# A two-layer hybrid encoder on one core: state-space maps issued in smaller steps, and sums, divisions and neighbours in the mixer rearranged

## The chip, the cores and the metric

The kernel runs on one core of a Trainium2 chip. The metric is device time in microseconds. The core has TensorE (PE in the rows, its weight loads PEld), VectorE (DVE), ScalarE (ACT), GpSimd (POOL) and SyncE (SP), which here only issues DMAs. Each engine works through a queue of its own, in order.

## The reference

The input x is 512 x 1024, float32; two layers, each with four residual steps, then a final RMSNorm:

```python
x = x + 0.5 * swiglu(rms_norm(x, ffn1_norm[i]), w_gate, w_up, w_down)     # d_ff = 2816
q, k, v, u = split(rms_norm(x, mix_norm[i]) @ w_in[i])                    # 512, 128, 128, 512 columns
attn = banded_attention(q, k, v, sink, bias)        # 8 heads, 2 kv heads, |i-j| <= 128, blocks of 128
ssm = s5_mixer(u, ...)                              # 32 groups of 16 channels, 64 complex states, 2 directions
x = x + concat(rms_norm(attn), rms_norm(ssm)) @ w_out[i]
x = x + 0.5 * swiglu(rms_norm(x, ffn2_norm[i]), ...)
```

The state-space mixer steps s_t = A s_(t-1) + B u_t and reads y_t = Re(C s_t), with a diagonal complex A for each group, once forwards and once backwards; y passes a GELU and a gated linear unit.

## The kernel before, in words

Activations are held transposed (channels on the 128 partitions, 512 tokens along the free axis). Float32 accuracy comes from three passes (`mm3`, L227 to L231): each weight chunk of 128 x 2048 is loaded to `raw`, ACT rounds it to `whi` (L212), and DVE or POOL subtracts to get `wlo` (L215), in halves of 1024 columns. `POOL_SPLIT` lists the halves that POOL takes, as (kind, first tile, half).

**The feed-forward blocks** (`ffn`, L364) run three groups of 8, 7 and 7 tiles of 128 hidden channels. A tile is 48 matmuls (gate and up, 8 x 3 each); after a group come 8 down tiles of 24 or 21. The down result is added to x (L421, L423), on POOL except in the last group.

**The maps of the state-space mixer** (`s5_steps`, L530) are computed from the parameters in the background of the feed-forward blocks. The function is a generator: each `yield` ends a step. `set_bg` (L164) gives it so many steps for so many points; a gate-and-up tile counts 3 points, a down tile 1, and `step` (L169) runs the generator until it has kept pace. Layer 0's generator (with the attention bias first) gets 224 steps for the 90 points of the first block, layer 1's 180 for 150 points of the two blocks between the mixers. What is left is drained before the mixer. In order, the generator makes scalars and powers, tables of cosines and sines (L669 to L694, POOL), and then eight units u (L717 to L777) of four groups. A unit makes, on POOL, the output map f (`fr`, `fi`, L734 to L737, from Cr, Ci and the powers pf) and the input map e (`er`, `ei`, L741 to L744, from four factors that DMAs have brought back from `bt` and `pt` in DRAM), 12 instructions on 128 x 512; e goes to `ed` in DRAM, f a unit later (`LAG = 1`) into TensorE products (L757, L764) with the padded B and then to `fd`.

**The mixer** (`mixer`, L800) runs the steps that `ORDER` (L45) lists by hand. `pu` projects u, `ui` brings it back from DRAM in another layout (8 DMAs a tile), `l` loads a quarter's input maps and tables (4 `ed`, 3 `tb` DMAs), `L` its output maps; `si` (L866) applies the input map on TensorE and rotates by the tables (L880 to L887), `sc` (L890) scans on DVE (L894) and rotates back (L897 to L908), `so` (L912) applies the output map. `k`, `v`, `vt` and `q` are the projections of attention, `as` the scores of a unit (block n, kv head) with the exponential on ACT, `an` the division of the probabilities (L1035), `ao` transposes them (L1043 to L1048), `pv` multiplies by v and squares for the norm (L1053 to L1076). `yt`, `glu` and `sn` end the state-space branch; `ws` and then `wa` are the two halves of the output projection (L1099, L1109), each adding to x at L1113; `ADD_V` says which of these adds are DVE's (first for ws, then for wa). After each wa add, `after(d)` prepares the next block's input (L290, L296, L301, L308).

The program is traced in this order, and a scheduler then fixes each engine's queue, taking what it expects to be ready first; so an engine's order in the trace need not be the program's. Activations and temporaries share one pool of slots that `slot` hands out (L105).

Of the kernel before, what the change touches and what calls it, by code (L numbers as in the profile page):

```python
# [12 lines left out]
AF = mybir.ActivationFunctionType  # L13
ALU = mybir.AluOpType
# [3 lines left out]
P = 128  # L18
# [27 lines left out]
l0 ui0 pu2 pu3 ui2 si0 ui1 k l1 ui3 v vt si1 L0 q0 sc0 sc1 l2 q1 si2 q2 l3 si3 sc2 q3 L1 L3 so0 L2 as0 an0  # L46
as1 so1 sc3 so2 so3 yt0 yt1 an1 as2 ao0 an2 as4 ao1 glu pv0 as3 ao2 sn ws0 an4 an3 ao3 ws1 as5 ws2 ao4 ws3
an5 as6 an6 ws4 ws5 ao5 pv1 as7 ws6 an7 ao6 pv2 ao7 ws7 pv3
""".split()

POOL_SPLIT = {("u", 0, 0), ("u", 0, 1), ("u", 2, 0), ("q", 0, 0), ("q", 0, 1), ("q", 2, 1), ("glu", 0, 1),
              ("ws", 0, 1), ("ws", 4, 0), ("wa", 0, 1), ("wa", 4, 1)}
# [3 lines left out]
ADD_V = ((0, 7), (5, 7))  # L56
# [22 lines left out]
class Emit:  # L79
# [450 lines left out]
    def s5_steps(self, l):  # L530
# [186 lines left out]
        for u in range(8 + LAG):  # L717
            if u < 8:
                g0 = u * 4
                fac = nxt  # L720

                def mat(x):
                    return x[:, g0 * 16:g0 * 16 + 64].rearrange("p (g o h) -> p g o h", g=4, o=1).to_broadcast([P, 4, 8, 16])

                def pwo(x, r):
                    return x[:, r, :, g0:g0 + 4].rearrange("p n (g o) -> p g n o", o=1).to_broadcast([P, 4, 8, 16])

                def full(x):
# [71 lines left out]
    def mixer(self, l, st, after):  # L800
# [65 lines left out]
        def s_in(q):  # L866
# [157 lines left out]
        def a_norm(n, kv):  # L1024
# [7 lines left out]
            for i in range(4):  # L1032
                hd = kv * 4 + i
                p = at[n]["p"][kv][:, i * T:i * T + nk]
                V.tensor_scalar(p, p, den[:, hd:hd + 1], None, op0=M)  # L1035

        def a_out(n, kv):
            k0, k1 = at[n]["k"]
            pp = at[n]["p"].pop(kv)
            for kb in range(k0, k1):  # L1040
# [4 lines left out]
                if kb % 2:  # L1045
# [7 lines left out]
        def a_pv(n):  # L1053
# [309 lines left out]
def plan_all(e):  # L1363
    st = new_st(GC_FFN1)
    e.setup(st)
    for l in range(L):
# [6 lines left out]
        if l == 0:  # L1373
            e.set_bg(prep(), 224, 90)
# [5 lines left out]
        if l + 1 < L:  # L1380
            e.set_bg(e.s5_steps(l + 1), 180, 150)
# [23 lines left out]
```

## Time and profile before

| | us |
|---|---|
| median of 3 runs | 1917.55 (1916.8 to 1920.2) |
| profiled execution, its own time | 1919.46 |
| its span, first to last instruction | 1917.7 |
| busy: TensorE, DVE, POOL, ACT | 1853.3, 1095.9, 690.9, 618.3 |

A time in a row counts from the start of the span. Layer 0's first block ends near 405 us, its mixer near 606; layer 1's mixer lies between about 1343 and 1540 us. Where a row ends in brackets, it gives the idle time just before the instruction and what ended it. "PEclk" is the granted clock of TensorE as a share of 2.4 GHz.

### The profile page before, as it was taken

The numbers are of one execution on the slowest core, as the hardware profiler recorded it, in microseconds if no ns is written. First come the engines' busy times: TensorE is split into PE (matmuls) and PEld (weight loads), VectorE is DVE, ScalarE is ACT, GpSimd is POOL, SyncE is SP. The second block draws the span as 40 slices with busy tenths as digits, with TensorE's granted clock in tenths as the row PEclk, the third lists the DMA queues.
The fourth block names the chain that finished last, engine by engine and source line by source line (L and its number), as shares of the span: only waits on it lengthen the run. The fifth ranks groups of instructions, "written<-read, shape, count | busy, mean of one in ns | idle before, by whom it ended". The sixth has DMA issues, their size and how long they took to land. (4 is left out here: it accounts for less than half of the span.)

```text
span 1917.7 us, 23722 instructions
## 1 busy us (share of the span) xinstructions
PE 1853.3 (97%) x9360; PEld 1500.3 (78%) x9360; DVE 1095.9 (57%) x1724; ACT 618.3 (32%) x932; POOL 690.9 (36%) x581
## 2 busy tenths in 40 slices
PE   8999997998999999999999999999989999999997
PEld 6888885887667888888888888888776678888886
DVE  7655542659876846345664444446598663434435
ACT  5222221332743322223332122224247442222223
POOL 2029878644244015074483551103343320201102
PEclk9999998999899999999999999999999999999998
DMA  5534546666221223334434433525650122232321
GB/s 203 165 123 140 178 158 204 187 241 221 72 69 66 109 88 140 110 115 160 157 144 149 173 134 103 152 88 184 199 179 23 66 86 91 88 107 83 107 96 47
DMA packets 95799, 249.46 MB, mean 130 GB/s; under 512 B 31768, under 2 KB 39112, under 8 KB 79944
## 3 DMA queue, kind: packets, MB, share of 16 engines
q1 hardware_dynamic: 94456, 246.86, 38.4%
q8 instruction: 73, 1.20, 0.3%
q10 hardware_dynamic: 1232, 1.09, 0.2%
q14 instruction: 38, 0.31, 0.0%
HBM read 217.89 MB, written 36.32 MB: 133 GB/s over the span
## 5 line engine op out<-in xcount | busy, mean ns | idle before, releaser
L229 PE MATMUL psum<-blk,whi 128*128 128x512 f32 (+1 forms) x2446 | 952.7, 391 | 11.6 <-ACT blk L290 6.5
L230 PE MATMUL psum<-blk,whi 128*128 128x512 f32 (+1 forms) x2446 | 952.2, 390 | 6.1 <-DVE blk L296 5.9
L231 PE MATMUL psum<-blk,wlo 128*128 128x512 f32 (+1 forms) x2446 | 951.2, 390 | 1.2 <-DVE wlo L215 1.2
L229 PEld LDWEIGHTS psum<-blk,whi 128*128 128x128 f32 x2446 | 460.5, 188 | 111.9 <-ACT blk L290 6.7
L230 PEld LDWEIGHTS psum<-blk,whi 128*128 128x128 f32 x2446 | 460.6, 188 | 104.2 <-DVE blk L296 10.7
L231 PEld LDWEIGHTS psum<-blk,wlo 128*128 128x128 f32 x2446 | 460.5, 188 | 96.1 <-DVE wlo L215 2.1
L212 ACT CAST whi<-raw 128x1024 fp32r<-128x1024 f32 (+1 forms) x310 | 303.3, 1027 | 714.3 <-PE psum L230 492.9
L215 DVE TENSOR_TENSOR wlo<-raw,whi 128x1024 fp32r<-128x1024 f32 (+1 forms) x288 | 411.9, 1463 | 83.7 <-ACT whi L212 74.8
L397 DVE TENSOR_TENSOR blk<-psum,blk 128x512 f32<-128x512 f32 x88 | 60.7, 691 | 315.0 <-PE psum L231 308.3
L423 POOL TENSOR_TENSOR xtile<-xtile,blk 128x512 f32<-128x512 f32 x64 | 92.5, 1447 | 392.9 <-DVE blk L421 344.1
L421 DVE SCALAR_TENSOR_TENSOR blk<-psum,blk 128x512 f32<-128x512 f32 x94 | 64.8, 690 | 190.8 <-PE psum L231 179.9
L396 ACT ACTIVATE blk<-blk 128x512 f32<-128x512 f32 x88 | 55.6, 632 | 325.3 <-DVE blk L394 321.4
L394 DVE TENSOR_TENSOR blk<-psum,blk 128x512 f32<-128x512 f32 x88 | 60.3, 689 | 107.4 <-PE psum L231 79.6
L215 POOL TENSOR_TENSOR wlo<-raw,whi 128x1024 fp32r<-128x1024 f32 x22 | 59.0, 2689 | 132.1 <-ACT whi L212 77.5
L308 POOL TENSOR_TENSOR blk<-blk,blk 128x512 f32<-128x512 f32 x30 | 46.3, 1543 | 132.5 <-ACT blk L301 131.8
L401 DVE TENSOR_TENSOR blk<-blk,blk 128x512 fp32r<-128x512 f32 x88 | 72.2, 822 | 0.1
L296 DVE SCALAR_TENSOR_TENSOR blk<-xtile,consts,blk 128x512 fp32r<-128x512 f32 x48 | 58.5, 1237 | 9.9 <-ACT blk L290 9.9
L1113 POOL TENSOR_TENSOR xtile<-xtile,blk 128x512 f32<-128x512 f32 x24 | 34.0, 1439 | 73.4 <-DVE blk L1111 73.4
L308 POOL TENSOR_TENSOR blk<-blk 128x512 f32<-128x512 f32 x11 | 17.5, 1591 | 110.8 <-issue 87.1
L735 POOL TENSOR_TENSOR blk<-blk,blk 128x512 f32<-128x512 f32 x32 | 44.1, 1380 | 30.5 <-DVE blk L401 26.1
L400 ACT CAST blk<-blk 128x512 fp32r<-128x512 f32 x88 | 54.1, 615 | 2.7 <-DVE blk L397 2.7
L290 ACT ACTIVATE blk<-xtile,consts 128x512 fp32r<-128x512 f32 x48 | 34.2, 719 | 51.5 <-DVE xtile L423 37.5
(235 smaller groups left out, 1388.3 us busy)
## 6 DMA issues: line engine op xcount, KB each, us to landing
raw<-w SPq DMA_DIRECT2D x123, 1024.0 KB
raw<-w SPq DMA_DIRECT2D x32, 896.0 KB
blk<-pt SPq DMA_DIRECT2D x32, 256.0 KB
blk<-bt SPq DMA_DIRECT2D x32, 256.0 KB
fd<-blk SPq DMA_DIRECT2D x32, 256.0 KB
ed<-blk SPq DMA_DIRECT2D x32, 256.0 KB
blk<-ed SPq DMA_DIRECT2D x32, 256.0 KB
blk<-fd SPq DMA_DIRECT2D x32, 256.0 KB
```

The lines of the kernel that those rows point to most:

```text
L212: self.S.copy(hi[:, c], raw[:, c])
L215: eng.tensor_tensor(out=lo[:, c], in0=raw[:, c], in1=hi[:, c].bitcast(F32), op=ALU.subtract)
L229: t.matmul(out, wh, xh, start=start, stop=False)
L230: t.matmul(out, wh, xl, start=False, stop=False)
L231: t.matmul(out, wl, xh, start=False, stop=stop)
L296: self.V.scalar_tensor_tensor(lo.bitcast(F32R), self.x[d], self.gains[:, st["g"] + d:st["g"] + d + 1], hi, op0=ALU.mult, op1=ALU.subtract)
L308: eng.tensor_tensor(out=acc, in0=acc, in1=sq, op=ALU.add)
L394: V.tensor_tensor(out=s, in0=pg, in1=R, op=ALU.mult)
L397: V.tensor_tensor(out=s, in0=pu, in1=s, op=ALU.mult)
L401: V.tensor_tensor(out=lo.bitcast(F32R), in0=s, in1=hi, op=ALU.subtract)
L421: V.scalar_tensor_tensor(t, ps, 0.5, R, op0=ALU.mult, op1=ALU.mult)
L423: (V if last else self.G).tensor_tensor(out=self.x[d], in0=self.x[d], in1=t, op=ALU.add)
```

## The change

In the maps, a unit makes e first and f after it; each of the 12 POOL instructions now ends with a yield of its own, f's slots are taken later, and the factor loads of the next unit are issued between e and f as before between e and the next unit's f. The steps given are 256 (layer 0) and 212 (layer 1). In the order, l1 moves behind ui3 and v, ws4 ahead of an6, pv1 behind as7, ws6 and an7, and ws7 behind pv3. Work changes engines: four sums of `si` go from POOL to DVE, five divisions a layer from DVE to ACT, the last sum of squares of n = 0 to DVE, three halves of weight splits from POOL to DVE; of the ws adds d = 0 and 7 go to POOL and d = 4 to DVE, and the wa adds d = 5 and 7 go to POOL. `G_SUM` and `V_PT` write out what the code did already.

```diff
-l0 ui0 pu2 pu3 ui2 si0 ui1 k l1 ui3 v vt si1 L0 q0 sc0 sc1 l2 q1 si2 q2 l3 si3 sc2 q3 L1 L3 so0 L2 as0 an0
+l0 ui0 pu2 pu3 ui2 si0 ui1 k ui3 v l1 vt si1 L0 q0 sc0 sc1 l2 q1 si2 q2 l3 si3 sc2 q3 L1 L3 so0 L2 as0 an0
 as1 so1 sc3 so2 so3 yt0 yt1 an1 as2 ao0 an2 as4 ao1 glu pv0 as3 ao2 sn ws0 an4 an3 ao3 ws1 as5 ws2 ao4 ws3
-an5 as6 an6 ws4 ws5 ao5 pv1 as7 ws6 an7 ao6 pv2 ao7 ws7 pv3
+an5 as6 ws4 an6 ws5 ao5 as7 ws6 an7 pv1 ao6 pv2 ao7 pv3 ws7

-POOL_SPLIT = {("u", 0, 0), ("u", 0, 1), ("u", 2, 0), ("q", 0, 0), ("q", 0, 1), ("q", 2, 1), ("glu", 0, 1),
-              ("ws", 0, 1), ("ws", 4, 0), ("wa", 0, 1), ("wa", 4, 1)}
+G_SIN = {(1, 1), (2, 0), (3, 0), (3, 1)}
+G_SUM = {(0, 1), (1, 1), (2, 1)}
+G_SQ = {(0, 0), (1, 0), (1, 1), (2, 0), (2, 1)}
+V_PT = {(0, 1), (0, 3), ... (7, 1), (7, 3)}
+S_DIV = {(3, 0), (3, 2), (5, 1), (6, 2), (7, 1)}
+POOL_SPLIT = {("glu", 0, 1), ("q", 0, 1), ("u", 0, 0), ("u", 0, 1), ("wa", 0, 1), ("wa", 4, 1), ("ws", 0, 1),
+              ("ws", 4, 0)}

-ADD_V = ((0, 7), (5, 7))
+ADD_V = ((4,), ())

-                fr, fi, er, ei, t = (self.slot() for _ in range(5))
+                er, ei, t = (self.slot() for _ in range(3))
                 M = ALU.mult
-                for o, a, b, sg in ((fr, Cr, Ci, ALU.add), (fi, Ci, Cr, ALU.subtract)):
-                    Gp.tensor_tensor(out=full(o), in0=mat(a), in1=pwo(pfv, 0), op=M)
-                    Gp.tensor_tensor(out=full(t), in0=mat(b), in1=pwo(pfv, 1), op=M)
-                    yield
-                    Gp.tensor_tensor(out=o, in0=o, in1=t, op=sg)
-                    yield
                 b0, b1, p0, p1 = fac
                 for r, (o, a, b, sg) in enumerate(((er, b0, b1, ALU.subtract), (ei, b1, b0, ALU.add))):
                     Gp.tensor_tensor(out=o, in0=a, in1=p0, op=M)
+                    yield
                     Gp.tensor_tensor(out=t, in0=b, in1=p1, op=M)
                     yield
                     Gp.tensor_tensor(out=o, in0=o, in1=t, op=sg)
                     SP.dma_start(out=ed[u // 2, :, r, u % 2 * T:u % 2 * T + T], in_=o)
                     yield
-                self.free(t, er, ei, *fac)
+                self.free(er, ei, *fac)
                 if u < 7:
                     nxt = factors(u + 1)
+                fr, fi = self.slot(), self.slot()
+                for o, a, b, sg in ((fr, Cr, Ci, ALU.add), (fi, Ci, Cr, ALU.subtract)):
+                    Gp.tensor_tensor(out=full(o), in0=mat(a), in1=pwo(pfv, 0), op=M)
+                    yield
+                    Gp.tensor_tensor(out=full(t), in0=mat(b), in1=pwo(pfv, 1), op=M)
+                    yield
+                    Gp.tensor_tensor(out=o, in0=o, in1=t, op=sg)
+                    yield
+                self.free(t)

-            Gp.tensor_tensor(out=s[0], in0=s[0], in1=s[1], op=A)
+            (Gp if (q, 0) in G_SIN else V).tensor_tensor(out=s[0], in0=s[0], in1=s[1], op=A)
-            Gp.tensor_tensor(out=s[2], in0=s[3], in1=s[2], op=B)
+            (Gp if (q, 1) in G_SIN else V).tensor_tensor(out=s[2], in0=s[3], in1=s[2], op=B)

-                V.tensor_scalar(p, p, den[:, hd:hd + 1], None, op0=M)
+                if (2 * n + kv, i) in S_DIV:
+                    S.activation(p, p, AF.Copy, scale=den[:, hd:hd + 1])
+                else:
+                    V.tensor_scalar(p, p, den[:, hd:hd + 1], None, op0=M)

-            e.set_bg(prep(), 224, 90)
+            e.set_bg(prep(), 256, 90)
-            e.set_bg(e.s5_steps(l + 1), 180, 150)
+            e.set_bg(e.s5_steps(l + 1), 212, 150)
```

## Rows read from the trace of the kernel before

**Rows 1.** The page, busy time, share of the span and instructions of TensorE.

```profile
PE 1853.3 (97%) x9360; PEld 1500.3 (78%) x9360; DVE 1095.9 (57%) x1724; ACT 618.3 (32%) x932; POOL 690.9 (36%) x581
```

**Rows 2.** TensorE's waits: waiting line, releaser, us in total, times, longest.

```profile
PE psum L757 <- POOL blk L737: 13.6, 2, 8.0
...
PE psum L1010 <- DVE blk L881: 6.4, 2, 3.2
...
PE psum L985 <- DVE blk L961: 5.0, 2, 3.3
...
PE psum L229 <- ACT blk L1069: 2.4, 2, 1.2
```

**Rows 3.** Busy time by stretch: length, PE, PEld, DVE, ACT, POOL, clock, DMA.

```profile
142.00:192.00 50.00, 50.00 (x222) 41.42 (x221) 24.93 (x25) 13.88 (x17) 48.91 (x78) 1.00 0.46 144
192.00:298.00 106.00, 106.00 (x581) 86.92 (x580) 49.32 (x46) 22.60 (x31) 86.35 (x62) 1.00 0.55 169
298.00:313.00 15.00, 1.36 (x18) 0.57 (x20) 3.84 (x3) 2.67 (x4) 12.49 (x12) 0.66 0.62 206
313.00:364.00 51.00, 50.41 (x319) 40.44 (x312) 27.05 (x27) 14.37 (x23) 45.47 (x32) 0.97 0.54 183
```

**Rows 4.** Timeline of TensorE, 302 to 313 us: start, us, then the operation.

```profile
303.96 0.65 PE L757 MATMUL psum<-blk,blk 128*32 128x128 f32 x8 [5.64 <-POOL blk L737]
312.61 0.66 PE L757 MATMUL psum<-blk,blk 128*32 128x128 f32 x8 [8.00 <-POOL blk L737]
```

**Rows 5.** The table by stretch again, right after the stall.

```profile
312.00:316.00 4.00, 3.39 (x30) 2.84 (x31) 0.00 (x0) 0.00 (x0) 2.70 (x3) 0.50 0.58 195
```

**Rows 6.** POOL's groups, 192 to 313 us: busy, mean ns, idle before.

```profile
L423 POOL TENSOR_TENSOR xtile<-xtile,blk 128x512 f32<-128x512 f32 x8 | 11.7, 1472 | 0.0
L741 POOL TENSOR_TENSOR blk<-blk,blk 128x512 f32<-128x512 f32 x8 | 11.4, 1425 | 13.1 <-DMA blk<-bt 10.9 <-issue 2.2
```

**Rows 7.** The table by stretch in layer 0's mixer and just before it.

```profile
430.00:488.00 58.00, 49.90 (x467) 40.16 (x467) 53.13 (x75) 14.36 (x20) 32.74 (x21) 0.90 0.67 220
536.00:560.00 24.00, 24.00 (x106) 15.85 (x104) 17.17 (x51) 8.82 (x24) 10.12 (x6) 0.93 0.12 44
392.00:424.00 32.00, 32.00 (x153) 26.76 (x152) 18.18 (x25) 9.13 (x13) 11.56 (x5) 1.00 0.74 264
```

**Rows 8.** Timeline of DVE in layer 0's mixer, 434 to 444 us.

```profile
435.66 2.29 DVE L894 TENSOR_TENSOR_SCAN blk<-blk,blk 128x511 f32<-128x511 f32 x1 [0.97 <-POOL blk L884]
...
438.12 0.69 DVE L903 TENSOR_TENSOR blk<-blk,blk 128x512 f32<-128x512 f32 x1
438.73 1.22 DVE L894 TENSOR_TENSOR_SCAN blk<-blk,blk 128x511 f32<-128x511 f32 x1
439.87 2.80 DVE L906 TENSOR_TENSOR blk<-blk,blk 128x512 f32<-128x512 f32 x1
...
443.80 1.21 DVE L215 TENSOR_TENSOR wlo<-raw,whi 128x1024 fp32r<-128x1024 f32 x1
```

**Rows 9.** Timeline of POOL, 439 to 442 us.

```profile
439.78 2.34 POOL L215 TENSOR_TENSOR wlo<-raw,whi 128x1024 fp32r<-128x1024 f32 x1 [2.91 <-ACT whi L212]
```

**Rows 10.** Timeline of SP's DMA issues in layer 1's mixer, 1372 to 1380 us.

```profile
1373.38 0.43 SPq L851 DMA_DIRECT2D blk<-ed  x1
1373.85 5.39 SPq L823 DMA_DIRECT2D blk<-ud  x8
```

**Rows 11.** Timeline of TensorE in layer 1's mixer, 1376 to 1382 us.

```profile
1378.96 0.45 PE L875 MATMUL psum<-blk,blk 128*64 128x64 f32 x6 [1.35 <-DMA blk<-ed]
1381.11 0.80 PE L985 MATMUL psum<-consts,blk 128*128 128x128 f32 x4 [1.71 <-DVE blk L961]
```

**Rows 12.** The page's groups: an ACT pass over 128 x 512.

```profile
L396 ACT ACTIVATE blk<-blk 128x512 f32<-128x512 f32 x88 | 55.6, 632 | 325.3 <-DVE blk L394 321.4
```

**Rows 13.** Timeline of POOL at the end of layer 0's mixer, 594 to 600 us.

```profile
594.76 5.51 POOL L1113 TENSOR_TENSOR xtile<-xtile,blk 128x512 f32<-128x512 f32 x4 [17.94 <-DVE blk L1111]
```

**Rows 14.** Timeline of DVE at the same place, 607 to 610 us.

```profile
607.54 1.77 DVE L1113 TENSOR_TENSOR xtile<-xtile,blk 128x512 f32<-128x512 f32 x1
```

More of the change, by code (lines that the diff above doesn't have):

```diff
@@ L45 @@
 ORDER = """
-l0 ui0 pu2 pu3 ui2 si0 ui1 k l1 ui3 v vt si1 L0 q0 sc0 sc1 l2 q1 si2 q2 l3 si3 sc2 q3 L1 L3 so0 L2 as0 an0
+l0 ui0 pu2 pu3 ui2 si0 ui1 k ui3 v l1 vt si1 L0 q0 sc0 sc1 l2 q1 si2 q2 l3 si3 sc2 q3 L1 L3 so0 L2 as0 an0
 as1 so1 sc3 so2 so3 yt0 yt1 an1 as2 ao0 an2 as4 ao1 glu pv0 as3 ao2 sn ws0 an4 an3 ao3 ws1 as5 ws2 ao4 ws3
-an5 as6 an6 ws4 ws5 ao5 pv1 as7 ws6 an7 ao6 pv2 ao7 ws7 pv3
+an5 as6 ws4 an6 ws5 ao5 as7 ws6 an7 pv1 ao6 pv2 ao7 pv3 ws7
 """.split()
-POOL_SPLIT = {("u", 0, 0), ("u", 0, 1), ("u", 2, 0), ("q", 0, 0), ("q", 0, 1), ("q", 2, 1), ("glu", 0, 1),
-              ("ws", 0, 1), ("ws", 4, 0), ("wa", 0, 1), ("wa", 4, 1)}
+G_SIN = {(1, 1), (2, 0), (3, 0), (3, 1)}
+G_SUM = {(0, 1), (1, 1), (2, 1)}
+G_SQ = {(0, 0), (1, 0), (1, 1), (2, 0), (2, 1)}
+V_PT = {(0, 1), (0, 3), (1, 1), (1, 3), (2, 1), (2, 3), (3, 1), (3, 3), (4, 1), (4, 3), (5, 1), (5, 3), (6, 1),
+        (6, 3), (7, 1), (7, 3)}
+S_DIV = {(3, 0), (3, 2), (5, 1), (6, 2), (7, 1)}
+POOL_SPLIT = {("glu", 0, 1), ("q", 0, 1), ("u", 0, 0), ("u", 0, 1), ("wa", 0, 1), ("wa", 4, 1), ("ws", 0, 1),
+              ("ws", 4, 0)}
 POOL_Q = ((2, 1), (3, 1))
-ADD_V = ((0, 7), (5, 7))
+ADD_V = ((4,), ())
 STARTX = ((0, 1), (1, 1), (2, 2), (4, 2), (6, 2))
@@ L904, in s_scan @@
             V.tensor_tensor(out=s[2], in0=s[3], in1=si, op=M)
-            both(V, rho, s[0], s[2], B)
+            both(Gp if (q, 0) in G_SUM else V, rho, s[0], s[2], B)
             V.tensor_tensor(out=s[1], in0=s[1], in1=si, op=M)
             V.tensor_tensor(out=s[3], in0=s[3], in1=co, op=M)
-            both(V if q == 3 else Gp, co, s[1], s[3], A)
+            both(Gp if (q, 1) in G_SUM else V, co, s[1], s[3], A)
             self.free(*s, si)
@@ L1044, in a_out @@
                 pt = self.slot()
-                if kb % 2:
+                if (2 * n + kv, kb) in V_PT:
                     V.tensor_copy(pt, b)
@@ L1072, in a_pv @@
             V.tensor_tensor(out=abuf[1][:, cs].bitcast(F32R), in0=f, in1=abuf[0][:, cs], op=B)
-            eng = V if n == 3 else Gp
-            eng.tensor_tensor(out=q[:, 0:256], in0=q[:, 0:256], in1=q[:, 256:512], op=A)
-            eng.tensor_tensor(out=acc_a[:, n * P:(n + 1) * P], in0=q[:, 0:P], in1=q[:, P:2 * P], op=A)
+            eng = [Gp if (n, i) in G_SQ else V for i in range(2)]
+            eng[0].tensor_tensor(out=q[:, 0:256], in0=q[:, 0:256], in1=q[:, 256:512], op=A)
+            eng[1].tensor_tensor(out=acc_a[:, n * P:(n + 1) * P], in0=q[:, 0:P], in1=q[:, P:2 * P], op=A)
             self.free(f, q, at[n]["sm"])
```

## The prediction

> **What bounds the kernel now.** First the page's busy line: TensorE counts 1853.3 us of a span of 1917.7 [rows 1], so 64.4 us are idle; only these, and stretches at a lowered clock, can be won. Next TensorE's waits [rows 2]: the largest that this change touches is that of L757 (the state-space maps' products) for POOL's sums in L737, 13.6 us in two waits; then, in the mixers, waits for DVE (L881, L961) and for ACT at L1069. The start and the end of the program make most of the rest, and the change leaves them alone.
>
> The table by stretch places the large wait: in 298 to 313 us TensorE is busy 1.36 us of 15, and POOL is nearly full from 142 us on: 48.91 of 50 us, 86.35 of 106, then 12.49 of 15 in the stall itself [rows 3]. TensorE's rows say the same: the fifth product (unit 4) waited 5.64 us for its real part and 8.00 for its imaginary part [rows 4]. Afterwards the granted clock is 0.50, the lower level of 1.2 GHz, in 312 to 316 us, with 3.39 us of TensorE work [rows 5], so 1.7 us more are lost. The stall's whole price is 13.6 + 1.7 = 15.3 us, once: layer 1's maps are spread over 150 points, not 90, and show no such wait.
>
> **Part 1: maps in smaller steps, input maps first.** No POOL instruction is added or removed (12 a unit, 8 units). What moves is when they are issued. Counting yields in layer 0: 26 for the bias, 51 to the tables, 32 for the tables, 2, then the units (88 before, 120 after), 14 at the end: 213 and 245. The pace is 224/90 = 2.49 and 256/90 = 2.84 steps a point, so all ends near point 86 in both. But the tables begin at 77/2.84 = 27.1 instead of 30.9 points, the units at 111/2.84 = 39.0 instead of 44.6. A point of a gate-and-up tile is 16 matmuls; at 222 matmuls in 50 us [rows 3] that is 3.6 us, and one of a down tile is 24, so 5.4 us. Both starts come some 20 us earlier (5.6 x 3.6; 3.8 x 5.4). Four more of the residual adds (L423) fall among the tables, some 5 us by their mean of 1472 ns [rows 6]; so POOL reaches the units about 15 us earlier, near 177 instead of 192 us. The small DVE work ahead of the tables gets 14% denser at the program's start; before, no wait of TensorE stands behind any of it, and without that slack the 5.6 points gained would shrink.
>
> POOL's own pace: from 192 to 313 us it did 64 instructions of the units in 121 us, 1.89 us each, the L423 and 22 us of idle time in it [rows 3], most of that for the factor loads from bt [rows 6]; after 313, 32 in 50 us, 1.56 us each [rows 3]. Before, 18 POOL instructions stand between a unit's last f product and the matmuls that take it (its own er and ei, and the next unit's 12); after, the next unit's 12, and for unit 7 none (six before). The matmuls' step is 127 + 11v before and 135 + 15v after (196 and 228 for unit 7). For unit 4 that is point 68.7 and 68.6, so TensorE still asks near 298 us. POOL is ready after 60 instructions: 177 + 60 x 1.89 = 290 us, 8 us in hand where 14 were missing. Unit 6: 290 + 24 x 1.56 = 327, asked at point 79.1, 298 + 10.5 x 3.6 = 336. Unit 7: 346, asked at point 80.2, 340: six late, of which the schedule, which sets a product where it expects the inputs, should take half. I take 3 us of new idle time and 0.3 for its clock: 15.3 - 3.3 = **12.0 us won**. Bounds: all 15.3; or, if 1.89 us held to the end, unit 7 at 177 + 96 x 1.89 = 358, 18 us late, 4.4 lost. Layer 1: 15 steps at 212/150 are 10.6 points, over 38 us a unit, against 12 x 1.89 = 23: nothing.
>
> **Part 2: the front of the mixer.** From 430 to 488 us DVE is busy 53.13 of 58 us [rows 7], and TensorE's waits for L881 and L961 are for its results, so here a us of DVE is a us of TensorE. Work goes to DVE: four sums (L884 for q 0 and 1, L887 for q 0 and 2) and three halves of weight splits. Yet POOL holds DVE up: L906 takes 2.80 us where the like L903 takes 0.69, and POOL's L215 of 2.34 us lies over it; the scan L894 takes 2.29 us beside a POOL sum and 1.22 without [rows 8, 9]. For one layer: the second half of q 2's split costs DVE 1.21 and frees 2.11: -0.9. Both sums of q 0: 2 x 0.69 added, the idle 0.97 ahead of the scan and its excess of 1.07 removed: -0.7. L884 of q 1: into a DVE wait, while the POOL sum that stays starts earlier and leaves the next scan alone: -0.3. L887 of q 2: +0.69, against an excess like the 1.07: -0.4. The first halves of q 0's and u 2's splits fall where DVE has room (18.18 of 32 us busy in 392 to 424 [rows 7]): nothing; without it, 1.2 each. That is -2.3 a layer, **4.6 us won**. Bounds: 6.4 + 5.0 = 11.4, all of the two waits; or, if POOL's holds only fall on other DVE work, 4 x 0.69 + 1.21 - 0.97 = 3.0 a layer, 6 lost.
>
> l1 moved: seven loads on SP's queue (4 ed, 3 tb) go behind ui3's eight, and on TensorE behind v's 24 matmuls. In layer 1 one ed load was issued only at 1373.38, just ahead of ui3's eight, which took 5.39 us of the queue [rows 10]; TensorE already waited 1.35 us for it, and 1.71 for the v result right after, till 1381.11 [rows 11]. Behind ui3 the load can be 5.4 us later, with 2.2 of cover: 3.2 lost at most; a gain is open if the slots come free earlier. I take **0.5 lost**, near the low end, since the loads that were prefetched early stay so. ui3 is not needed before si3.
>
> **Part 3: the mixer's end.** ws7's 12 matmuls (2.7 us) now follow pv3, for whose result L1069 the first wa product waited up to 1.2 us, 2.4 in both layers [rows 2]: **2.4 won**; as cover for unit 7's divisions, which ws7 was, pv1 steps in. ws4 ahead of an6 puts its product and its DVE add before four divisions that only ao6 awaits: nothing. Five divisions a layer go from DVE to ACT, busy 8.82 of 24 us in 536 to 560 [rows 7]: nothing; were ACT full, each would delay its transposes by an ACT pass, some 0.6 us [rows 12]. The second sum of squares of n = 0 goes to DVE, and the ws adds swap engines, both far ahead of need: nothing. The two wa adds, d = 5 and 7, go to POOL. On POOL one takes 5.51/4 = 1.38 us there [rows 13], on DVE one took 1.77 [rows 14]: zero, between 0.4 won and, if the last queues behind one POOL add, 1.4 lost, a layer. The Trainium skill (GPSIMD Engine Reference, Key points) holds DVE about twice as fast in elementwise work; by that rule the four adds would cost an estimated 2.8 us more and the sum would end at 1902. No row here shows these adds at that gain.
>
> Sum: -12.0 - 4.6 + 0.5 - 2.4 = -18.5. The profiled execution took 1919.46 us, 1.8 more than its span, and stands 1.9 above the median of 1917.55; from the median the forecast is **1899 us**.
>
> **Rivals.** (a) *Factor loads at the head of each unit; slower.* er is now a unit's first work and needs the loads at once. POOL idled 22 us in 64 instructions, 4.2 a unit. If that doubles, unit 7 is ready 33 us later, at 380 against 340: 40 idle instead of 13.6, 1.7 more for the clock, 6.5 won elsewhere: 1917.55 + 26.4 + 1.7 - 6.5 = 1939 us. It ends slower than before once the added wait passes 1.8 us a unit. For it: the waits exist. Against: six POOL instructions, 8 us or more, stand between issue and use in both orders, and fewer slots are held. (b) *The stall only moves to unit 7*, by the pace of 1.89: + 4.4 - 6.5, 1915. (c) *DVE becomes the bound in the front*, its new work not paid back: -12 + 6 + 0.5 - 2.4, 1910. (d) *The change does little*: an engine's order is the scheduler's, not the list's; in the trace vt's transposes stand inside si1 [rows 11]. Then 1917.
>
> **How the numbers follow.** Forecast 0.66 (1889 to 1907 by itself), (a) 0.08, (b) 0.08, (c) 0.13, (d) 0.05. The likeliest gives 1899. For 8 in 10 the range runs from 1887 (all of the stall and most of the front's bound) to 1915, which takes in (c) and (b). About 0.2%, 3.8 us, is what a measurement of this kernel can tell from no change: forecast and (c) are faster, 0.79; (b) and (d) the same, 0.13; (a) slower, 0.08.
>
> **What would show it.** Right: no wait of L757 near 298 us, at most a short one near 340; POOL full from about 121 us on; L906's like at 0.69 us; no wait of wa for L1069. Wrong: TensorE idle over 10 us between 330 and 380 us (a, b); DVE's front stretch as long as before (c); a longer wait for ed in layer 1 (part 2).

## The result, and the profile after

| | before | after |
|---|---|---|
| median, us | 1918.13 (4 runs, 1916.8 to 1920.2) | 1886.66 (4 runs, 1884.87 to 1887.72) |
| ratio | | 0.9834, interval 0.9817 to 0.9851 |
| span of the profiled run, us | 1917.7 | 1885.9 |

The forecast was 1899 with a range of 1887 to 1915: the direction was right, the gain of 31.5 us is 13 more than the 18.5 forecast, and the time lies 0.3 us below the range.

The page's busy line of the changed kernel, beside [rows 1]. TensorE is idle 37.8 us instead of 64.4, and its busy time is 5.2 shorter with the same 9360 matmuls; the mean granted clock of the profiled run is 0.992 instead of 0.987.

```profile
PE 1848.1 (98%) x9360; PEld 1497.6 (79%) x9360; DVE 1103.9 (59%) x1724; ACT 624.7 (33%) x942; POOL 686.1 (36%) x571
```

TensorE's waits after, beside [rows 2]. Lines have moved: L771 is the old L757, L889 the old L875 (`si`), L895 and L975 the old L881 and L961, L1086 the old L1069, L306 the old L296.

```profile
PE psum L889 <- DMA blk<-ed: 5.2, 4, 1.6
...
PE psum L1024 <- DVE blk L895: 4.0, 2, 2.1
PE psum L239 <- ACT blk L1086: 2.2, 2, 1.1
PE psum L240 <- DVE blk L306: 2.0, 3, 0.7
...
PE psum L771 <- POOL blk L761: 0.7, 1, 0.7
```

The 13.6 us for POOL's sums are 0.7. The wait for the v result (L961) is gone, and ed loads are waited for four times. The wait for L1069, which ws7 was to cover, is still there.

Where the gain arises can be read without a model: `mm3` issues 7338 matmuls in both kernels, in nearly the same order (149 places hold another of the three passes), so the start of the nth can be compared (the 1450th starts at 369.9 before and at 355.6 after). Each line gives the gain within a stretch. The second column takes another run of each kernel (e0_before and g0_after, below), so it shows how far a single trace carries.

| stretch, up to the nth of these matmuls | first traces | second traces | forecast |
|---|---|---|---|
| start and layer 0's first block, 1450 | 14.3 | 14.2 | 12.0 |
| mixer of layer 0, front, 1850 | 4.9 | 5.0 | 2.3 |
| its middle, 2000 | 3.2 | 1.4 | 0 |
| its end, 2150 | 2.8 | 2.8 | 1.2 |
| the blocks between, 4900 | 1.1 | 1.1 | 0 |
| mixer of layer 1, front, 5500 | 1.8 | 5.3 | 2.3 - 0.5 |
| its middle, 5650 | 0.9 | 0.9 | 0 |
| its end, 5800 | 2.8 | 2.8 | 1.2 |
| sum | 31.8 | 33.5 | 18.5 |

**The maps.** Busy time by stretch after (length, PE, PEld, DVE, ACT, POOL, clock, DMA), beside [rows 3]; then POOL's first and last unit rows after, and the same two before.

```profile
169.00:275.00 106.00, 104.74 (x543) 85.38 (x543) 51.57 (x48) 26.12 (x34) 80.39 (x58) 1.00 0.54 176
275.00:290.00 15.00, 15.00 (x96) 12.25 (x95) 9.15 (x9) 4.45 (x7) 14.92 (x10) 1.00 0.39 115
290.00:341.00 51.00, 50.27 (x279) 41.02 (x278) 28.31 (x24) 13.61 (x20) 49.59 (x35) 1.00 0.55 187
```

```profile
152.33 1.29 POOL L757 TENSOR_TENSOR blk<-blk,blk 128x512 f32<-128x512 f32 x1
...
341.94 2.01 POOL L761 TENSOR_TENSOR blk<-blk,blk 128x512 f32<-128x512 f32 x1
```

```profile
175.36 1.12 POOL L734 TENSOR_TENSOR blk<-blk,blk 128x512 f32<-128x512 f32 x1
...
361.17 1.62 POOL L744 TENSOR_TENSOR blk<-blk,blk 128x512 f32<-128x512 f32 x1
```

The first unit instruction comes 23 us earlier; it stands alone in both kernels, and the dense run of them starts at 166.68 instead of 192.68, 26 earlier (forecast 15). They end at 344 (forecast 346 for the last f). TensorE is busy 50.27 of 51 us in 290 to 341, where before 15 us held 1.36 of work. What is left is one short wait, near 324 us (TensorE's products after; the first row is unit 4's, the second unit 5's second half, the last two are units 6 and 7):

```profile
300.44 0.64 PE L771 MATMUL psum<-blk,blk 128*32 128x128 f32 x16
...
324.27 0.32 PE L771 MATMUL psum<-blk,blk 128*32 128x128 f32 x4 [0.73 <-POOL blk L761]
...
346.74 0.65 PE L771 MATMUL psum<-blk,blk 128*32 128x128 f32 x16
...
347.33 0.62 PE L771 MATMUL psum<-blk,blk 128*32 128x128 f32 x16
```

POOL's first unit row in the changed kernel is L757, a product of f: the scheduler mixes e and f on POOL in both kernels. "e first" is the order in which the program takes slots and issues loads and stores, and not POOL's order.

**The mixer's end.** DVE and POOL after, beside [rows 13, 14]; then what TensorE waits for there, after and before.

```profile
575.17 3.23 DVE L306 SCALAR_TENSOR_TENSOR blk<-xtile,consts,blk 128x512 fp32r<-128x512 f32 x2
...
572.35 8.92 POOL L1130 TENSOR_TENSOR xtile<-xtile,blk 128x512 f32<-128x512 f32 x6 [15.10 <-DVE blk L1128]
...
555.99 0.50 PE L239 MATMUL psum<-blk,whi 128*128 128x512 f32 x1 [1.12 <-ACT blk L1086]
...
591.44 0.50 PE L240 MATMUL psum<-blk,whi 128*128 128x512 f32 x1 [0.72 <-DVE blk L306]
```

```profile
607.68 0.50 PE L230 MATMUL psum<-blk,whi 128*128 128x512 f32 x1 [1.46 <-DVE blk L296]
...
611.05 0.50 PE L230 MATMUL psum<-blk,whi 128*128 128x512 f32 x1 [1.71 <-DVE blk L296]
```

The two waits of 3.17 us in all are one of 0.72. They are waits for the input splits (`x_lo`, L296), which on DVE stood behind the wa adds. On POOL the adds are waited for by ACT, which rounds their result (ACT's waits in 560 to 630 us after); TensorE's one wait there stays the 0.72.

```profile
ACT blk L300 <- POOL xtile L1130: 7.8, 5, 3.2
```

### The profile page after: what moved, and what is told of

It is laid out like the page before. It is cut to its first block, busy times and chain, and to the rows that moved or that the text cites. A ratio compares the mean times of both kernels' runs of the same rounds, so it can differ in the third digit from the quotient of the medians.

```text
span 1885.9 us, 23705 instructions
## 1 busy us (share of the span) xinstructions
PE 1848.1 (98%) x9360; PEld 1497.6 (79%) x9360; DVE 1103.9 (59%) x1724; ACT 624.7 (33%) x942; POOL 686.1 (36%) x571
## 4 chain that ended last, share of the span: by engine, by line
PE 83%; DVE 7%; DMA 3%; POOL 3%; issue 1%; SPq 1%; ACT 1%; DVEq 0%; POOLq 0%; ACTq 0%
PE psum L240 26%; PE psum L239 26%; PE psum L241 26%; PE psum L1075 1%; DVE wlo L225 1%; DMA ed<-blk 1%; DVE blk L306 1%; PE psum L1025 1%; DVE blk L908 1%; PE psum L1060 1%; DMA blk<-bt 1%; PE psum L349 1%; PE psum L1024 1%; SPq L837 1%; POOL blk L745 1%
## 5 line engine op out<-in xcount | busy, mean ns | idle before, releaser
L225 DVE TENSOR_TENSOR wlo<-raw,whi 128x1024 fp32r<-128x1024 f32 (+1 forms) x294 | 418.9, 1457 | 52.3 <-ACT whi L222 43.6
L433 POOL TENSOR_TENSOR xtile<-xtile,blk 128x512 f32<-128x512 f32 x64 | 95.5, 1493 | 370.6 <-DVE blk L431 362.6
L225 POOL TENSOR_TENSOR wlo<-raw,whi 128x1024 fp32r<-128x1024 f32 x16 | 41.3, 2584 | 140.4 <-ACT whi L222 140.3
L411 DVE TENSOR_TENSOR blk<-blk,blk 128x512 fp32r<-128x512 f32 x88 | 76.9, 876 | 0.1
L1130 POOL TENSOR_TENSOR xtile<-xtile,blk 128x512 f32<-128x512 f32 x30 | 45.6, 1545 | 69.0 <-DVE blk L1128 61.6
L306 DVE SCALAR_TENSOR_TENSOR blk<-xtile,consts,blk 128x512 fp32r<-128x512 f32 x48 | 62.8, 1333 | 10.6 <-ACT blk L300 9.8
L757 POOL TENSOR_TENSOR blk<-blk,blk 128x512 f32<-128x512 f32 x32 | 45.6, 1430 | 16.8 <-PE psum L771 11.9
```

Of the source, the lines that this page charges most:

```text
L225: eng.tensor_tensor(out=lo[:, c], in0=raw[:, c], in1=hi[:, c].bitcast(F32), op=ALU.subtract)
L306: self.V.scalar_tensor_tensor(lo.bitcast(F32R), self.x[d], self.gains[:, st["g"] + d:st["g"] + d + 1], hi, op0=ALU.mult, op1=ALU.subtract)
L411: V.tensor_tensor(out=lo.bitcast(F32R), in0=s, in1=hi, op=ALU.subtract)
L433: (V if last else self.G).tensor_tensor(out=self.x[d], in0=self.x[d], in1=t, op=ALU.add)
```

## The experiments

Ratios are to the kernel before, run on the same chip; "us" is (ratio - 1) x 1918. The changed kernel stands at 0.9834 and, run again, 0.984, -31 us. First the parts alone on the kernel before, then the changed kernel with a part taken back.

| kernel | ratio | interval | us |
|---|---|---|---|
| e1_maps: maps alone | 0.9938 | 0.9923 to 0.9954 | -11.9 |
| g1_first: e before f alone | 1.0062 | 1.0047 to 1.0077 | +11.9 |
| g2_steps: smaller steps alone | 0.9969 | 0.9955 to 0.9983 | -5.9 |
| e2_front: sums and splits alone | 0.9961 | 0.9946 to 0.9976 | -7.5 |
| h1_gsin: sums alone | 1.0027 | 1.0015 to 1.0038 | +5.2 |
| h2_split: splits alone | 0.9987 | 0.9977 to 0.9997 | -2.5 |
| e3_order: ORDER alone | 0.9994 | 0.9985 to 1.0004 | -1.2 |
| e4_adds: ws and wa adds alone | 0.9964 | 0.9948 to 0.9979 | -6.9 |
| k2_wa: wa adds alone | 0.9988 | 0.9972 to 1.0003 | -2.3 |
| e5_divs: divisions, squares alone | 0.9992 | 0.9977 to 1.0006 | -1.5 |
| f1_old_maps: after, old maps | 0.9917 | 0.9897 to 0.9936 | -15.9 |
| f2_old_order: after, old ORDER | 0.987 | 0.9852 to 0.9888 | -24.9 |
| f5_l1old: after, l1 ahead of ui3 | 0.9887 | 0.9872 to 0.9901 | -21.7 |
| f4_l1: after, l1 behind ui3 | 0.9855 | 0.984 to 0.987 | -27.8 |
| f3_old_adds: after, old adds | 0.9872 | 0.9849 to 0.9896 | -24.6 |
| k1_oldsin: after, sums on POOL | 0.9869 | 0.9849 to 0.9889 | -25.1 |

### The maps: e1_maps, f1_old_maps, g1_first, g2_steps

e1_maps and f1_old_maps swap the whole hunk of `s5_steps` and the two step counts. The other two split it, each on the kernel before:

```diff
 g1_first: er, ei first, then fr, fi; two products a step; 224 and 180 steps
 g2_steps: fr, fi first, as before, but
                     Gp.tensor_tensor(out=full(o), in0=mat(a), in1=pwo(pfv, 0), op=M)
+                    yield
...
-            e.set_bg(prep(), 224, 90)
+            e.set_bg(prep(), 256, 90)
... (the same yield in e; 180 becomes 212)
```

Expected of e1_maps: 

> The kernel before with the maps' part alone (e before f, a yield after each POOL instruction, 256 and 212 steps). If the parts stand for themselves: the wait of L757 near 298 us is gone, the first block ends 14 us earlier, and the time is 1904 us (1902 to 1906). If the stall's end needed the mixer's parts too, or the stall moved to unit 7, less than 5 us is won: 1913 or more. If the maps also carry what was won in the second half of layer 0's mixer (through other slots and another schedule), the time is 1898 or less.

Expected of f1_old_maps: 

> The changed kernel with the maps part alone undone (f before e, one step for two products, 224 and 180 steps). Alone, the maps won 10.3 us, with some 4 us given back near 82 us by a late weight half that the whole change does not show. Theory (the parts add up, the loss near 82 us is an accident of that combination): 13 to 15 us slower than the changed kernel, 1900 to 1902 us, with TensorE waiting 13 to 14 us for POOL's sums near 300 us again and nothing else moved. Rival (the maps in small steps also pay in the mixers of both layers): 18 us or more slower, and the mixer's stretches longer too.

Expected of g1_first: 

> The kernel before with only the order inside a unit of the maps changed: input maps (er, ei) first, the f products after, two products still in one step, 224 and 180 steps. Theory (what removed the stall is that the tables and the units begin some 15 us earlier on POOL, which comes from the larger number of steps, not from the order): TensorE still waits for POOL near 300 us, 10 to 25 us, since the f products of a unit now come six POOL instructions (some 11 us) later; as slow as before or up to 10 us slower. Rival (the order is what does it: factor loads get the six f instructions as cover, and POOL no longer idles for them): the wait falls below 5 us, 8 to 12 us faster.

Expected of g2_steps: 

> The kernel before with only the smaller steps of the maps: one product a step, 256 and 212 steps, f products first as before. Theory: the units begin some 15 us earlier, the stall near 300 us is gone or under 3 us, and the late weight half near 82 us costs 4 to 6 us as in three of the four kernels with the new maps; 8 to 12 us faster. Rival (the order does it): the stall stays at 10 us or more and the time stays within 4 us of before.

The maps win 12 us alone and 15 in company. e1_maps missed its 1902 to 1906 us (1909.9, with its before at 1920.1): it gives back 4 us near 82 us, see below. f1_old_maps came out by its theory, a little over: 15 to 16 us slower than the changed kernel, with TensorE waiting 10.9 us for POOL's sums again. The two halves of the maps don't add up: e before f alone loses 12, smaller steps alone win 6, together they win 12. g1_first came out as its theory had it, somewhat worse than its upper end (TensorE waits 12.9 us for POOL's sums). g2_steps missed: it won 6, not 8 to 12, because a stall stayed in another form. TensorE's waits of g2_steps, then POOL's waits in 150 to 365 us of g2_steps, then SP's there; then POOL's and SP's for e1_maps, which differs from g2_steps in the order inside a unit alone (f's later slots with it), and for the changed kernel:

```profile
PE psum L229 <- ACT whi L212: 7.2, 1, 7.2
...
POOL blk L744 <- DMA blk<-bt: 26.8, 3, 11.5
POOL blk L742 <- DMA blk<-pt: 11.4, 5, 3.8
...
SPq L747 <- POOL blk L746: 76.0, 16, 16.3
SPq L775 <- POOL blk L738: 52.6, 14, 12.3
```

```profile
POOL blk L745 <- DMA blk<-bt: 12.1, 3, 6.5
...
SPq L750 <- POOL blk L749: 48.0, 14, 9.0
...
SPq L787 <- POOL blk L761: 24.4, 8, 6.7
```

```profile
POOL blk L745 <- DMA blk<-bt: 10.9, 3, 6.0
...
SPq L750 <- POOL blk L749: 48.0, 13, 9.6
...
SPq L787 <- POOL blk L761: 23.9, 8, 6.7
```

SP's issues stand in one chain in these traces: a store of e or f on it waits for POOL's sum, and the loads of the next factors, and of the next weights, stand behind. With smaller steps alone the stores hold the queue 129 us (76.0 + 52.6) and POOL then idles 38 us for factors; with e first as well it is 72 and 12 (e1_maps; 72 and 11 in the changed kernel). In the kernel before it is 88 and 17, and with e first alone 70 and 16. So the order inside the unit gets the stores off SP's queue sooner, which pays only with the earlier start. That these holds are what makes the loads late is read from the waits; neither they nor the slots held by f were tried by themselves.

Three of the kernels with the new maps (e1_maps, f2_old_order, f3_old_adds) lose 4 to 6 us near 82 us in their traces; f5_l1old loses 4 there too, f4_l1 2, the changed kernel's second trace 1, k1_oldsin nothing. The view is SP's issues, ACT's casts and TensorE's wait, f3_old_adds first, then after:

```profile
51.84 5.26 SPq L701 DMA_DIRECT2D tb<-blk  x1
57.19 1.75 SPq L208 DMA_DIRECT2D raw<-w  x1
...
82.33 1.99 ACT L222 CAST whi<-raw 128x1024 fp32r<-128x1024 f32 x2 [15.02 <-DMA raw<-w]
...
83.42 0.79 PE L239 MATMUL psum<-blk,whi 128*128 128x512 f32 x1 [2.49 <-ACT whi L222]
```

```profile
51.53 4.52 SPq L701 DMA_DIRECT2D tb<-blk  x1
56.15 1.94 SPq L208 DMA_DIRECT2D raw<-w  x1
...
78.70 2.00 ACT L222 CAST whi<-raw 128x1024 fp32r<-128x1024 f32 x2 [11.39 <-DMA raw<-w]
```

Before, the weight's load went out at 51.45 us; with the new pace a table store of the maps, tb, goes ahead of it. In all of these kernels the load goes out at 56.0 to 57.2 us, and its cast starts 22 to 25 us later; in the changed kernel it is just in time. Why one of them gets it later than another, though the edits of f2, f3 and f5 lie in the mixers, is open. This is near the risk that the prediction named ("small DVE work ahead of the tables gets 14% denser"), but on SP's queue and not on DVE, and it is a large part of what f2, f3 and f5 lose: 4.0 of 6.6 us at the 2150th matmul in f2, 5.7 of 8.0 in f3.

### The front of the mixer: e2_front, h1_gsin, h2_split, k1_oldsin

```diff
 h1_gsin: on the kernel before
+G_SIN = {(1, 1), (2, 0), (3, 0), (3, 1)}
 h2_split: on the kernel before
-POOL_SPLIT = {("u", 0, 0), ("u", 0, 1), ("u", 2, 0), ("q", 0, 0), ("q", 0, 1), ("q", 2, 1), ...
+POOL_SPLIT = {("glu", 0, 1), ("q", 0, 1), ("u", 0, 0), ("u", 0, 1), ...
 e2_front: both
 k1_oldsin: on the changed kernel, all eight (q, i) in G_SIN
```

Expected of e2_front: 

> The kernel before with four sums of si and three halves of the splits on DVE, nothing else. If DVE is relieved by more than it is given: 2.3 us a layer by the end of si, 1913.5 us (1911 to 1915.5). If its work is not paid back: 1918 to 1924. If the relief also lifts the granted clock of the next stretch in layer 0: 1908 or less, with layer 0's mixer shorter by 5 us or more and layer 1's by about 2.5.

Expected of h1_gsin: 

> The kernel before with only the sums of the mixer's front moved between POOL and DVE (G_SIN; G_SUM lists what POOL had but for q 2, which goes to DVE's side as in the changed kernel). By the prediction's terms the sums win 0.7 + 0.3 + 0.4 = 1.4 us a layer, 2.8 in all. Theory (as the prediction had it): 2 to 4 us faster. Rival (it is the weight splits that hold DVE up): within 1.5 us of before.

(Other than this text says, G_SUM moves nothing, for q 2 either: it writes out what the code did.)

Expected of h2_split: 

> The kernel before with only the three halves of weight splits moved from POOL to DVE. By the prediction's terms: 0.9 us a layer from q 2's second half, nothing from the two others, 1.8 in all. Theory: 1 to 3 us faster, and the DVE instruction that took 2.80 us beside POOL's split takes 0.7. Rival (DVE is full and its new halves of 1.2 us each delay the products that TensorE waits for): 2 us slower or more.

Expected of k1_oldsin: 

> The changed kernel with all eight sums of the mixer's front back on POOL. Alone on the kernel before, the four moved sums lost 5 us; with the splits moved as well, the pair won 6.7 against the splits' 2.5. Theory (the sums pay only together with the splits: with POOL's splits still in the way, DVE takes on sums and is held up all the same): 3 to 5 us slower than the changed kernel. Rival (the sums cost DVE what they cost, 0.69 us each, and e2_front's gain came from a stretch of full clock): as fast or up to 3 us faster.

The sums alone lose 5 us, the splits alone win 2.5, both win 7.5 (e2_front, costed at 4.6), and in the changed kernel the sums are worth 6. So h1_gsin went against theory and rival, h2_split came out by its theory in time, and k1_oldsin by its theory, a little over. By place, h1_gsin's two fronts are 2.4 and 4.6 us longer than in the first trace of the kernel before, and k1_oldsin's 2.9 and 2.5 longer than in that of the changed kernel. TensorE in h1_gsin's front (timeline), then DVE and POOL there:

```profile
462.45 0.84 PE L885 MATMUL psum<-blk,blk 128*64 128x64 f32 x18 [3.73 <-DVE blk L986]
...
467.97 0.80 PE L885 MATMUL psum<-blk,blk 128*64 128x64 f32 x10 [3.93 <-DMA blk<-ed]
```

```profile
460.04 3.96 DVE L986 TENSOR_TENSOR blk<-blk,blk 64x512 fp32r<-64x512 f32 x2
...
459.44 2.34 POOL L225 TENSOR_TENSOR wlo<-raw,whi 128x1024 fp32r<-128x1024 f32 x1
```

With the sums on DVE while POOL keeps its splits, DVE is late with the low halves of q (L986, 3.96 us for two with a POOL split over them; TensorE waits 3.7 us), and the ed loads come late as well. A single DVE instruction beside a POOL split is held as before: 2.74 us in h1_gsin's trace. That this, and not the late ed loads, is what turns the sums' gain into a loss is not shown. In the changed kernel the front shows both halves of the prediction's reading, one right and one wrong (DVE and POOL after, beside [rows 8, 9]):

```profile
434.83 2.83 DVE L908 TENSOR_TENSOR_SCAN blk<-blk,blk 128x511 f32<-128x511 f32 x2
...
441.59 2.25 DVE L913 TENSOR_TENSOR blk<-blk,blk 64x512 f32<-64x512 f32 x1
...
440.86 2.44 POOL L225 TENSOR_TENSOR wlo<-raw,whi 128x1024 fp32r<-128x1024 f32 x1 [5.39 <-ACT whi L222]
```

Two scans now take 2.83 us where one took 2.29 beside a POOL sum. But a POOL split, now glu's, still lies over a DVE sum, and holds it 2.25 us where 0.68 would do.

### The order: e3_order, f2_old_order, f4_l1, f5_l1old

```diff
 f5_l1old: on the changed kernel; f2_old_order takes back the rest of the list too
-... ui1 k ui3 v l1 vt si1 ...
+... ui1 k l1 ui3 v vt si1 ...
 f4_l1: on the changed kernel
+... ui1 k ui3 l1 v vt si1 ...
```

Expected of e3_order: 

> The kernel before with the new order alone (l1, ws4, pv1 and ws7 moved). If ws7 covers the wait for L1069 as the prediction said: 2.4 us won less 0.5 for the ed load, 1915.5. If the scheduler sets ws7 elsewhere, since the wait stands in the changed kernel too: 1918, within 1. If l1's loads come late: 1919 to 1922, with a longer wait for ed in layer 1. If pv1's new place is what lets layer 0's second half run at the full clock: 1913 or less.

Expected of f2_old_order: 

> The changed kernel with the old ORDER list. The new list alone won 0.7 us, within what can be told from nothing. Theory (the list is worth nothing by itself but is what lets the freed DVE time reach TensorE: v's matmuls ahead of l1 and vt's transposes before si1): 5 to 8 us slower than the changed kernel, TensorE's waits for the v result back at 3 to 5 us in both layers. Rival (the list is worth nothing in either company; what it wins in vt's wait it loses in waits for ed): within 2 us of the changed kernel, the waits for ed 3 us shorter and some other wait as much longer.

Expected of f4_l1: 

> The changed kernel with l1 between ui3 and v, its loads still behind ui3's on SP's queue, its slots taken before v's. The changed kernel's trace has four waits for ed loads, 5.2 us in all, two a layer. Theory (the loads go out as their slots come free and as the queue reaches them; v's place does not matter to either): within 2 us of the changed kernel, waits for ed 4 to 6 us. Rival (behind v the loads wait for slots that v's products hold): waits for ed under 3 us and 2 to 3 us faster than the changed kernel.

Expected of f5_l1old: 

> The changed kernel with l1 at its old place, ahead of ui3. Theory (ui3's eight loads, some 5 us of the queue, are what made the ed loads late): the waits for ed fall from 5.2 to under 2.5 us, and the v result is waited for again at most 1 us, since DVE no longer holds it up; 1 to 3 us faster than the changed kernel. Rival (l1's old place brings back the wait of vt for the v result of 1.7 to 3.3 us a layer): 2 to 4 us slower than the changed kernel.

Alone the list is worth nothing that can be told; TensorE's wait for the v result is gone in e3_order too, and its front of layer 1 is no shorter for it. In company l1's place is all of it: f5_l1old is as slow as f2_old_order. But 4 of the 6 to 10 us are those near 82 us, ahead of any mixer. In the mixers, front and middle, the traces leave 0.8 to 1.4 us in layer 0 and 0.8 to 3.6 in layer 1, by which trace of the changed kernel they are held against. The waits for ed depend little on l1's place: 5.2 us in the changed kernel, 5.0 in f2_old_order, 6.1 in f5_l1old, 5.7 in f4_l1. So f5_l1old's theory and f2_old_order's rival, that they would shrink with l1 in its old place, were wrong, and the wait for the v result, which f2's theory and f5's rival had as the price, did not come back in either. f4_l1's theory had the waits right, but the kernel is some 3 us slower than the changed one, 2 of them near 82 us. In f2_old_order and f5_l1old, TensorE waits 5.7 and 5.6 us for DVE's L895 instead of 4.0 (4.4 in g0_after); that is the part of the later l1's gain that can be named. No kernel here beats the changed one.

### The adds: e4_adds, f3_old_adds, k2_wa

```diff
-ADD_V = ((0, 7), (5, 7))
+ADD_V = ((4,), ())
```

(k2_wa: `((0, 7), ())`.)

Expected of e4_adds: 

> The kernel before with the output projection's adds changed alone (ws: d 4 on DVE; wa: none on DVE). By the prediction nothing, 1917 to 1920. If the time between the last product and the next block came from DVE waiting out POOL's adds, as the waits of the changed kernel suggest (L240 for L306 2.0 us against 5.9 before): 2 to 2.5 us a layer, 1913.5. By the rule that POOL is twice as slow: 2.8 lost, 1921.

Expected of f3_old_adds: 

> The changed kernel with the adds behind the ws and wa products on the engines of before (ws 0 and 7, wa 5 and 7 on DVE). Theory (the last wa adds on POOL shorten the end of each mixer, since DVE there also makes the input splits of the next feed-forward block, held up by POOL's own adds): 2.4 us a layer slower, some 5 us, 1891 to 1893, with the first matmuls of the next block waiting 1.2 to 1.9 us twice for the input splits. Rival (alone the adds won 7.0 us because of a stretch at a lower clock in the first mixer that the changed kernel does not have; the adds themselves are worth nothing, as the prediction had it): within 2 us of the changed kernel.

Expected of k2_wa: 

> The kernel before with only the two wa adds (d = 5 and 7) moved from DVE to POOL. Theory: on DVE each of these adds, 1.78 us beside POOL, stands ahead of input splits of the next block that TensorE waits for 1.5 to 1.7 us twice; on POOL it runs beside them. The two waits fall to 0.7 us, 2 to 3 us a layer, 4 to 6 us faster in all. Rival (the ws adds, or a lower clock at 552 us that some runs do not have, made e4_adds' 7.0 us): within 2 us of before.

By place the three agree. From the 2000th to the 2150th matmul e4_adds and k2_wa gain 2.1 us on before, and in layer 1's end 2.8 each; f3_old_adds loses 2.8 at each end on the changed kernel. All twenty traces of this document fall in two groups there: 40.4 to 40.5 us for each end with the wa adds on DVE, 37.6 to 38.4 with them on POOL. By time k2_wa missed its 4 to 6 us: its total of -2.3 has an interval that takes in zero and the 4.9 of the two ends. What e4_adds won beyond k2_wa has no place in the ends, and no cause here; f3_old_adds was slower than its 1891 to 1893 us by what it lost near 82 us. TensorE at that place in k2_wa, beside 1.46 and 1.71 before:

```profile
611.21 0.50 PE L240 MATMUL psum<-blk,whi 128*128 128x512 f32 x1 [0.73 <-DVE blk L306]
...
612.89 0.50 PE L240 MATMUL psum<-blk,whi 128*128 128x512 f32 x1 [0.71 <-DVE blk L306]
```

The same DVE add, first with POOL idle, then with POOL's adds running beside it (timeline of DVE, f3_old_adds):

```profile
562.34 0.68 DVE L1130 TENSOR_TENSOR xtile<-xtile,blk 128x512 f32<-128x512 f32 x1
...
581.84 1.78 DVE L1130 TENSOR_TENSOR xtile<-xtile,blk 128x512 f32<-128x512 f32 x1
```

### The rest: e5_divs, g0_after, e0_before

```diff
 e5_divs: on the kernel before
+S_DIV = {(3, 0), (3, 2), (5, 1), (6, 2), (7, 1)}
+G_SQ = {(0, 0), (1, 0), (1, 1), (2, 0), (2, 1)}
```

Expected of e5_divs: 

> The kernel before with only the five divisions a layer on ACT and the second sum of squares of n = 0 on DVE. The other parts, each alone, have won 10.3 (maps), 6.7 (front), 7.0 (adds) and 0.7 us (order), 24.7 in all, and the whole change 31.5: nearly 7 us are unaccounted for. Theory (the prediction's step: costed at nothing, DVE has room there, and the missing 7 us are an interaction of parts): within 2 us of before. Rival (the missing 7 us are the divisions: DVE is what TensorE waits for at the transposes of the probabilities and at the input splits behind them): 5 to 7 us faster, with the waits of TensorE for DVE's divisions and input splits inside the mixer shorter.

Expected of g0_after: 

> The changed kernel itself again. Three of the four kernels with the new maps lost 4 to 6 us near 82 us, where a weight's raw load landed 2.8 to 3.6 us later than in the changed kernel's trace, behind a table load on SP's queue. If that is a matter of the run (of when the DMA engines get to the load), this run shows it too in some executions: 1890 to 1893 us. If it belongs to the kernels, the changed kernel stays at 1885 to 1888 us with no wait of TensorE for a weight half near 82 us.

Expected of e0_before: 

> The kernel before itself again, for its trace. In the first trace the granted clock was 0.79 from 552 to 560 us, in the first mixer's end, with TensorE busy all 8 us; it cost some 3.3 us, and four of the eight variants show no such stretch there. If it belongs to the kernel before, it stands here again at the same place; if it is a matter of the run, it is missing or stands elsewhere (the second mixer's end near 1480 to 1490 us).

e5_divs is the same as before, as costed. g0_after ran 1886.55 to 1890.58 us, 0.984 of before; near 82 us its trace shows waits of 0.27 and 0.52 us, so the weight's load is on the edge there, not clear of it. e0_before ran 1920.03 us, and the lower clock at 552 us was not there: it belonged to that run. (The 3.3 us of the expectation is the length of that stretch; at half the clock it cost 1.7.)

## Why the prediction was right and wrong

The time fell just below the range mainly because three terms of the sum were too small: the wa adds, put at 0, gave 5.6 us; the front with l1, put at 4.1, gave 6.7 to 10.3; the maps, put at 12.0, gave some 15. A fourth, ws7, was put at 2.4 and gave nothing; that it made up for part of the wa adds at the same place was luck.

**Maps, 12.0: right in mechanism, 2 to 3 short.** The earlier start (larger, 26 us for 15), the end of the units (344 for 346) and the vanished stall came as worked out. Unit 4's products, forecast at 298 us with their sums ready at 290, stand at 300.4, and the tenth of f's sums, two a unit, is done at 295.9. The 3 us of new idle time set aside for unit 7 were not needed: units 6 and 7 stand together at 346.7, behind the last sum at 344.0, and wait for nothing; the 0.7 left is unit 5's. What the step missed is why the two halves need each other: it counted POOL's instructions between issue and use by the program's order, and not SP's queue. Rival (a), slower by the factor loads, had the place right and the sign wrong for the whole change: POOL's idle time for factors went from 17 us to 11 instead of doubling. For e first alone, which loses 12 us, the sign was right, but POOL's idle time for factors, 16 us, did not grow; TensorE's 12.9 us for POOL's sums there are as g1_first's theory had them. Layer 1, "nothing", was 1.1: with the whole of the new maps the stretch between the mixers takes 634.95 us in every trace, with the old ones 636.0.

**Front, 4.6, and l1, -0.5: undersized.** The fronts gave 6.7 and 10.3 us in two pairs of traces. The step added terms one by one (0.7, 0.3, 0.4, 0.9), and the runs show that they are no terms: sums +5 alone and -6 in company. Its own reading of DVE, "L906's like at 0.69 us", failed, since another split took the place of q's. The wait for v, counted only as a bound, went entirely; the waits for ed came, as feared, and rose by 3.3 us (1.9 to 5.2), but they are there with either place of l1. Rival (c), DVE's new work not paid back, fell for the whole part; of the sums alone it is what h1_gsin shows.

**ws7, 2.4: wrong.** The wait for L1069 stays at 2.2 us, 1.1 in each layer, in the changed kernel and in e3_order, and the mixer's end is as long in e3_order as before. A list's order is not the engine's: pv3's matmuls, and two small ones of the norm, are still the last before wa. The prediction held this against itself, as rival (d), for the whole change, and not for this term.

**wa adds, 0: wrong by 5.6 us** (4.9 on the kernel before). It compared the add's 1.77 us on DVE with 1.38 on POOL and called it even. The price of an instruction on DVE there is what stands behind it: two adds of 1.78 us ahead of the splits that TensorE waits for. On POOL they stand ahead of nothing that TensorE waits for longer than 0.72 us. The Trainium skill (GPSIMD Engine Reference, Key points) holds DVE about twice as fast in elementwise work: the trace agrees for an add alone (0.68 us on DVE above, 1.29 to 1.49 on POOL), and the time went the other way. The same section says that POOL shares SBUF interfaces with DVE where DVE has two SBUF inputs; the 1.78 us of the same add beside POOL's agree.

**Divisions, squares, ws4, 0: right** (e5_divs, and no other trace speaks against ws4).

**Not forecast: clock.** 1.7 us of the first pair's gain lie in a stretch at clock 0.79 before that e0_before lacks. The 0.9 to 1.5 in each mixer's middle is in both pairs; its cause is open.

## What to carry to other kernels

Cost a moved instruction by what queues behind it on either engine, not by its duration there; and where stores and loads share an issuing queue, look for stores that wait for their data there, and for the loads behind them. Parts that trade work between two busy engines don't add up: take one back in the finished kernel as well as trying it alone. A hand-written order is a wish; read the engine's order in the trace before giving a swap a price.

## What the runs showed of the hardware

TensorE's granted clock fell once without a gap in TensorE's records. Busy time by stretch (length, PE, PEld, DVE, ACT, POOL, clock, DMA), first before, then e0_before, the same program:

```profile
552.00:560.00 8.00, 8.00 (x26) 3.31 (x24) 4.70 (x20) 3.17 (x14) 1.67 (x2) 0.79 0.27 111
```

```profile
552.00:560.00 8.00, 8.00 (x32) 4.20 (x31) 5.48 (x21) 4.12 (x17) 2.55 (x2) 1.00 0.38 131
```

The same view after, then of g0_after:

```profile
1376.00:1392.00 16.00, 12.32 (x137) 9.10 (x137) 15.78 (x27) 4.83 (x7) 8.31 (x6) 0.85 0.64 200
1392.00:1400.00 8.00, 8.00 (x68) 7.22 (x66) 7.97 (x18) 1.68 (x4) 4.98 (x4) 0.50 0.85 306
```

```profile
1376.00:1392.00 16.00, 13.78 (x142) 10.51 (x140) 15.77 (x28) 4.82 (x7) 8.28 (x5) 0.90 0.62 199
1392.00:1400.00 8.00, 8.00 (x83) 6.71 (x85) 7.97 (x17) 2.28 (x6) 5.60 (x4) 0.78 0.87 309
```

At 552 us TensorE counted as busy throughout, and the clock fell to a mean of 0.79 between its two levels in one run and not in the other. At 1392 us, after a stretch in which TensorE was busy 12.32 and 13.78 of 16 us, it stayed at the lower level of 1.2 GHz all 8 us in one run and for less than half of them in the other. Layer 1's front gained 1.8 us in the first pair of traces and 5.3 in the second. So a single trace tells a mixer's stretch only to within 2 to 3.5 us, and the gain by place was read from two pairs.
